# Where the softmax scale is multiplied in: from VectorE to POOL's rounding and a ScalarE copy

## The chip, the cores and the metric

The kernel runs on one core of a Trainium2 chip. TensorE (PE) multiplies matrices, VectorE (DVE), ScalarE (ACT) and GpSimd (POOL) work elementwise, and SyncE's queue (SP) issues the DMAs. The metric is the device time of one execution in microseconds (us), given as the median of several runs; one further execution was profiled.

## The reference

One layer of a streaming encoder over 1024 positions of width 1024, all in float32. A normalized, modulated input is projected once; the columns feed two groups of eight attention heads, whose outputs are joined and projected again, and a gated MLP follows. Both groups end in the same two steps, here for the first of them:

```python
s = jnp.where(mask[None, None], s, NEG_INF)
p = jax.nn.softmax(s, axis=-1).astype(v.dtype)
return jnp.einsum('bhqk,bkhd->bqhd', p, v)
```

The first group (latent attention, names with m) sees all earlier chunks of 64 positions. The second (band attention, names with c) sees a band of nine chunks and adds a bias that depends on the distance.

## The kernel before

Attention is cut into tiles of 128 query rows of one head. Eight heads by eight row blocks make 64 tiles of band attention and then 64 of latent attention, in `tiles`, half a head at a time (`Unit`). `scores` makes the probabilities of a tile, `values` multiplies those of two tiles by the values, three tiles behind. Between them `pace` and `need` draw pieces of other work from `fillers`: projections of later heads, the latent up-projections and the output projection of the band heads.

For a tile, `scores` does this, in order:

- TensorE writes the negated scores into one of two score banks (lines 822 and 829).
- VectorE takes the row minimum (840 and 844 for band tiles, which also adds the bias; 847 for latent ones).
- ScalarE takes the exponential into `P`, with the row sum in `rsum` as accumulator output (854). It appears in the profile as an activation and an accumulator read.
- VectorE takes the reciprocal `ri` of the sum (856) and multiplies it in place by `PSCALE`, 2 to the 15th (857).
- The probabilities, times `ri`, are split into two float16 halves side by side in `hl`. POOL rounds the product to the high half (`scale_pool`, line 74, called from the branch `mode == "1"`, which both mode strings choose for every piece). VectorE forms the product again and subtracts the high half, which leaves the low one (876). A latent tile of more than 512 columns is split in two pieces, so there are 64 band and 96 latent roundings.
- A DMA issued by SyncE transposes `hl` into `PT` (888), which `values` reads (916). Line 925 and 926 then join the two halves of the result.

`P` has three buffers, `hl` four and `rsum`, `ri` and `m` four each, one column wide.

The program is written in one stream. A planner orders it when the kernel is built: it plays the instructions through a model of their times and puts each engine's instructions into the order in which they come up there, by dependence and priority. Scores, the scaling and rounding, and the values each get a raised priority (`OFF_S`, `OFF_P`, `OFF_V`). On the chip every engine keeps the order that was written for it and waits where an input isn't ready.

Of the kernel before, what the change touches and what calls it, by code (L numbers as in the profile page):

```python
# [13 lines left out]
F32 = mybir.dt.float32  # L14
# [4 lines left out]
AF = mybir.ActivationFunctionType  # L19
# [3 lines left out]
MUL, ADD, SUB, MIN, MAX = ALU.mult, ALU.add, ALU.subtract, ALU.min, ALU.max  # L23

P = 128
# [21 lines left out]
PSCALE, VSCALE = 2.0 ** 15, 2.0 ** 14  # L47
# [18 lines left out]
def layer_kernel(ctx, tc, I, out):  # L66
    nc = tc.nc
    pe, act, dve, pool, sp = nc.tensor, nc.scalar, nc.vector, nc.gpsimd, nc.sync
# [4 lines left out]
    def scale_pool(o, i, s):  # L73
        pool.tensor_scalar(o, i, s, 1.0, op0=MUL, op1=MUL)  # L74
# [12 lines left out]
    cst = ctx.enter_context(tc.tile_pool(name="cst", bufs=1))  # L87
# [60 lines left out]
    def pgtile(shape, dt, name):  # L148
        return apg.tile(shape, dt, name=name, tag="pg", bufs=6)
# [642 lines left out]
    class Unit:  # L792
# [7 lines left out]
        def scores(u, i):  # L800

            qpg, kpgs = u.pages()
            bias = u.bias() if u.band else None
            lo = max(0, i - 4) if u.band else 0
            n = (i - lo + 1) * P
            nm = f"{u.nm}_{i}"
            rsum = cst.tile([P, 1], F32, name=f"rs{nm}", tag="rsum", bufs=4)
            ri = cst.tile([P, 1], F32, name=f"ri{nm}", tag="ri", bufs=4)
            with tc.high_priority(offset=OFF_S):
                s = ps.tile([P, 1024], F32, name=f"s{nm}", tag="S", bufs=2)  # L810
                n0 = max(0, min(4, i + 1) - lo) * P
                n1 = n - n0
                c0 = 512 - n0 if n1 else 0
                segs = [(c0, lo * P, n0, 0)] if n0 else []
                if n1:
                    segs.append((512, max(lo, 4) * P - 512, n1, 1))
                q = slice((i % 4) * P, (i % 4 + 1) * P)
                if u.band:
                    qh, ql = qpg
                    for x, a in enumerate((qh[u.odd], ql[u.odd])):  # L820
                        for c, ko, w, kh in segs:
                            last = pe.matmul(s[:, c:c + w], a[:, q], kpgs[kh][:, u.odd, ko:ko + w],
                                             start=(x == 0), stop=(x == 1))
                else:
                    for a in range(2):
                        for c, ko, w, kh in segs:
                            for b in range(2 - a):
                                rr = slice(0, QK if a or b else QK + NT)
                                last = pe.matmul(s[:, c:c + w], qpg[a][rr, q], kpgs[kh][rr, b, ko:ko + w],  # L829
                                                 start=(a == 0 and b == 0), stop=(a == 1))  # L830
                trail.append(last.ins)
                sv = s[:, c0:c0 + n]
                m = cst.tile([P, 1], F32, name=f"m{nm}", tag="m", bufs=4)
                if u.band:
                    if i >= 4:
                        dve.memset(sv[64:128, 0:64], BIG)
                    w = min(n, 256)
                    if n > 256:
                        m0 = cst.tile([P, 1], F32, name=f"m0{nm}", tag="m0", bufs=4)
                        dve.tensor_reduce(m0[:], sv[:, :n - 256], axis=AX.X, op=MIN)  # L840
                        init = m0[:]
                    else:
                        init = 3e38
                    anchor["dve"] = dve.tensor_tensor_reduce(sv[:, n - w:n], sv[:, n - w:n], bias[:, 256 - w:256], 1.0, init,  # L844
                                             ADD, MIN, accum_out=m[:]).ins
                else:
                    anchor["dve"] = dve.tensor_reduce(m[:], sv, axis=AX.X, op=MIN).ins  # L847
                short = n <= (640 if u.band else 512)
                pieces = [(0, n)] if short else [(0, 512), (512, n)]
                if n <= 640:  # L850
                    pr = at.tile([P, 640], F32, name=f"P{nm}", tag="P", bufs=P_BUFS)
                else:
                    pr = pgtile([P, 1024], F32, f"P{nm}")
                act.activation(pr[:, :n], sv, AF.Exp, bias=m[:], scale=-1.0, accum_out=rsum[:, 0:1])  # L854
            with tc.high_priority(offset=OFF_P):
                dve.reciprocal(ri[:], rsum[:, 0:1])
                dve.tensor_scalar(ri[:], ri[:], PSCALE, None, op0=MUL)  # L857
                for x, (p0, p1) in enumerate(pieces):
                    w = p1 - p0
                    cnt[0] += 1  # L860
                    if not u.band and cnt[0] % 4 == 0:
                        hl = apg.tile([P, 1024], F16, name=f"hl{nm}_{x}", tag="v16", bufs=3)
                    else:
                        hl = at.tile([P, 1280], F16, name=f"hl{nm}_{x}", tag="HL", bufs=HL_BUFS)
                    pp = pr[:, p0:p1]
                    mode = (MODE_C if u.band else MODE_M)[cnt[0] % 4]
                    if mode == "2":
                        scale_pool(pp, pp, ri[:])
                        act.activation(hl[:, :w], pp, AF.Copy)
                        pool.tensor_tensor(hl[:, w:2 * w], pp, hl[:, :w], op=SUB)  # L870
                    else:
                        if mode == "1":
                            scale_pool(hl[:, :w], pp, ri[:])
                        else:
                            act.activation(hl[:, :w], pp, AF.Copy, scale=ri[:])
                        dve.scalar_tensor_tensor(hl[:, w:2 * w], pp, ri[:], hl[:, :w], op0=MUL, op1=SUB)  # L876
                    nb = 10 if u.band else 8
                    if i % 2 == 0:
                        pair[0] += 1
                        if u.band or pair[0] % 2:  # L880
                            tt = at.tile([P, 20, P], F16, name=f"PT{nm}_{x}", tag="PT", bufs=2)
                        else:
                            tt = apg.tile([P, 16, P], F16, name=f"PT{nm}_{x}", tag="v16", bufs=3)
                        u.pt[i, x] = tt, {}
                    tt, where = u.pt[i - i % 2, x]
                    b0 = (i % 2) * nb
                    with tc.issue_after(anchor["om"]) if u is units[-1] and i == 7 else contextlib.nullcontext():
                        anchor["sp"] = sp.dma_start_transpose(tt[:, b0:b0 + 2 * w // P, :], hl[:, :2 * w]).ins
                    for j in range(w // P):
                        where.setdefault(lo + p0 // P + j, []).append((b0 + j, b0 + j + w // P, i % 2))  # L890
            return sum(3 * max(107, w / 2.4) for _, _, w, _ in segs)
# [789 lines left out]
```

## Time and profile before

| | us |
|---|---|
| median of 3 runs | 1311.97 |
| lowest and highest | 1311.38, 1319.53 |
| profiled execution, its own time | 1312.59 |
| span in the profile | 1310.8 |
| TensorE busy | 1189.1 (91%) |
| VectorE busy | 1075.0 (82%) |
| ScalarE busy | 625.8 (48%) |
| POOL busy | 597.9 (46%) |

In the profile a line names engine, source line, output and inputs; buffer numbers are left out, so `hlc` stands for the `hl` tiles of band attention and `hlm` for those of latent attention, `ric` and `rim` for their reciprocals. "PEld" is the loading of weights into TensorE. In a group, the count is followed by busy time and mean duration in ns, and then by the idle time of the engine just before such instructions, with what ended it. In a timeline each line gives the start and the duration in us. PEclk is the clock granted to TensorE as a share of its full speed.

### The profile page before, as it was taken

The numbers are of one execution on the slowest core, as the hardware profiler recorded it, in microseconds if no ns is written. First come the engines' busy times: TensorE is split into PE (matmuls) and PEld (weight loads), VectorE is DVE, ScalarE is ACT, GpSimd is POOL, SyncE is SP. The second block draws the span as 40 slices with busy tenths as digits, with TensorE's granted clock in tenths as the row PEclk, the third lists the DMA queues.
The fourth block names the chain that finished last, engine by engine and source line by source line (L and its number), as shares of the span: only waits on it lengthen the run. The fifth ranks groups of instructions, "written<-read, shape, count | busy, mean of one in ns | idle before, by whom it ended". The sixth has DMA issues, their size and how long they took to land. (4 is left out here: it accounts for less than half of the span.)

```text
span 1310.8 us, 18660 instructions
## 1 busy us (share of the span) xinstructions
PE 1189.1 (91%) x6168; PEld 988.0 (75%) x6168; DVE 1075.0 (82%) x1800; ACT 625.8 (48%) x1148; POOL 597.9 (46%) x639
## 2 busy tenths in 40 slices
PE   3899998889767889878989999999999999999998
PEld 3789888878545667656778888888888886888886
DVE  6979988888589778875899889888888987687667
ACT  5454654455567454543474443444453353433331
POOL 5485773587688534445515444544445441000000
PEclk9899999989889998988999999999999999999999
DMA  8416758766224777679503333343333337943451
GB/s 323 150 50 154 177 141 189 158 161 123 51 70 85 161 162 149 147 161 357 231 0 112 97 125 116 119 128 107 105 121 111 122 105 267 395 135 102 129 161 64
DMA packets 223688, 190.82 MB, mean 146 GB/s; under 512 B 148708, under 2 KB 166372, under 8 KB 223592
## 3 DMA queue, kind: packets, MB, share of 16 engines
q1 hardware_dynamic: 223592, 189.64, 51.4%
q8 instruction: 48, 0.79, 0.3%
q14 instruction: 48, 0.39, 0.1%
HBM read 117.50 MB, written 37.49 MB: 118 GB/s over the span
## 5 line engine op out<-in xcount | busy, mean ns | idle before, releaser
L78 ACT ACTIVATE dnP<-dnr 128x1024 fp32r<-128x1024 f32 x73 | 77.5, 1065 | 116.3 <-PE dnA_P L1492 46.3
L1464 DVE TENSOR_TENSOR dnP<-dnr,dnP 128x1024 fp32r<-128x1024 f32 x72 | 88.3, 1230 | 51.3 <-ACT dnP L78 51.3
L74 POOL TENSOR_SCALAR hlm<-Pm,rim 128x512 f16<-128x512 f32 (+3 forms) x96 | 67.5, 712 | 73.4 <-DVE rim L857 20.2
L85 POOL TENSOR_TENSOR wf<-wu,wf 128x512 fp32r<-128x512 f32 x22 | 39.6, 1798 | 116.6 <-ACT wf L78 116.6
L85 POOL TENSOR_TENSOR wb<-wu,wb 128x512 fp32r<-128x512 f32 x22 | 43.8, 1993 | 84.8 <-ACT wb L78 57.1
L876 DVE SCALAR_TENSOR_TENSOR hlm<-Pm,rim,hlm 128x512 f16<-128x512 f32 (+3 forms) x96 | 72.3, 769 | 12.4 <-POOL hlm L74 12.1
L829 PE MATMUL sm<-kp,qp 96*128 96x512 f32 (+7 forms) x288 | 70.0, 370 | 10.8 <-ACT Pm L854 7.7
L1326 DVE SCALAR_TENSOR_TENSOR u<-c,cvp,u 128x1023 f32<-128x1023 f32 x44 | 55.8, 1310 | 27.6 <-ACT u L1325 26.2
L854 ACT ACTIVATE Pm<-sm,mm 128x128 f32<-128x128 f32 (+3 forms) x64 | 47.3, 740 | 44.7 <-DVE mm L847 35.4
L74 POOL TENSOR_SCALAR hlc<-Pc,ric 128x640 f16<-128x640 f32 (+2 forms) x64 | 48.8, 765 | 42.8 <-DVE ric L857 14.7
L854 ACT ACTIVATE Pc<-sc,mc 128x640 f32<-128x640 f32 (+2 forms) x64 | 42.3, 662 | 51.4 <-DVE mc L844 28.6
L829 PEld LDWEIGHTS sm<-kp,qp 96*128 96x128 f32 (+1 forms) x288 | 48.0, 195 | 21.9 <-ACT Pm L854 12.3
L1325 ACT ACTIVATE u<-c,cvp 128x1024 f32<-128x1024 f32 x44 | 52.4, 1240 | 23.4 <-DVE c L1424 16.5
L916 PE MATMUL pvm<-PTm,vt 128*128 128x256 f16 (+1 forms) x320 | 42.6, 279 | 19.7 <-DMA PTm<-hlm 17.1
L876 DVE SCALAR_TENSOR_TENSOR hlc<-Pc,ric,hlc 128x640 f16<-128x640 f32 (+2 forms) x64 | 52.5, 827 | 8.5 <-POOL hlc L74 8.3
L78 ACT ACTIVATE wc<-ws 128x512 fp32r<-128x512 f32 x21 | 13.3, 634 | 92.9 <-DVE ws L1174 87.1
L1327 DVE SCALAR_TENSOR_TENSOR u<-c,cvp,u 128x1022 f32<-128x1022 f32 x44 | 55.5, 1302 | 0.0
L155 PE MATMUL ipq<-wq_s,hT 128*128 128x256 f32 x192 | 55.5, 289 | 0.0
L916 PEld LDWEIGHTS <-vt 128*128 128x128 f16 x320 | 30.1, 103 | 33.3 <-issue 20.5
L157 PE MATMUL ipq<-wq_s,hT 128*128 128x256 f32 x192 | 54.6, 284 | 0.0
L156 PE MATMUL ipq<-wq_s,hT 128*128 128x256 f32 x192 | 54.6, 284 | 0.0
L1491 PE MATMUL dnA_P<-dnP 128*128 128x512 f32 x132 | 51.3, 389 | 0.0
(436 smaller groups left out, 4376.0 us busy)
## 6 DMA issues: line engine op xcount, KB each, us to landing
wu<-w_up SPq DMA_DIRECT2D x44, 512.0 KB, 3.6
dnr<-g_d SPq DMA_DIRECT2D x73, 256.0 KB, 2.8
aw<-w_ada SPq DMA_DIRECT2D x48, 256.0 KB, 3.2
g_d<-u SPq DMA_DIRECT2D x22, 512.0 KB, 3.0
dnr<-w_down SPq DMA_DIRECT2D x44, 256.0 KB, 5.4
adaw<-w_ada_a SPq DMA_DIRECT2D x16, 512.0 KB, 6.4
x<-x SPq DMA_DIRECT2D x16, 512.0 KB, 9.1
g_d<-gs SPq DMA_DIRECT2D x22, 256.0 KB, 2.8
```

The lines of the kernel that those rows point to most:

```text
L74: pool.tensor_scalar(o, i, s, 1.0, op0=MUL, op1=MUL)
L78: act.activation(o, i, AF.Copy)
L85: (pool if eng == "p" else dve).tensor_tensor(o, i, f32(hi), op=SUB)
L155: pe.matmul(pt, sh, mh, start=(start and i == 0), stop=False)
L156: pe.matmul(pt, sh, ml, start=False, stop=False)
L829: last = pe.matmul(s[:, c:c + w], qpg[a][rr, q], kpgs[kh][rr, b, ko:ko + w], start=(a == 0 and b == 0), stop=(a == 1))
L854: act.activation(pr[:, :n], sv, AF.Exp, bias=m[:], scale=-1.0, accum_out=rsum[:, 0:1])
L876: dve.scalar_tensor_tensor(hl[:, w:2 * w], pp, ri[:], hl[:, :w], op0=MUL, op1=SUB)
L916: last = pe.matmul(dst, u.vst(j), mov, start=(x == 0), stop=(x == len(todo) - 1), skip_group_check=True)
L1326: dve.scalar_tensor_tensor(u[:, 1:], c[:, :S - 1], cvp[:, cv + 1:cv + 2], u[:, 1:], op0=MUL, op1=ADD)
L1327: dve.scalar_tensor_tensor(u[:, 2:], c[:, :S - 2], cvp[:, cv:cv + 1], u[:, 2:], op0=MUL, op1=ADD)
L1464: r = f(*a, **k)
```

## The change

The scale is no longer multiplied into `ri` by VectorE. POOL's rounding takes the unscaled reciprocal and, as its second factor, the constant `PSCALE` in place of 1.0. ScalarE copies `ri` times `PSCALE` into a new one-column tile `rp` with four buffers, and VectorE's low halves read `rp` in place of `ri`. Since the constant is a power of two, both orders of multiplying give the same numbers.

```diff
             with tc.high_priority(offset=OFF_P):
                 dve.reciprocal(ri[:], rsum[:, 0:1])
-                dve.tensor_scalar(ri[:], ri[:], PSCALE, None, op0=MUL)
+                rp = cst.tile([P, 1], F32, name=f"rp{nm}", tag="rp", bufs=4)
+                act.activation(rp[:], ri[:], AF.Copy, scale=PSCALE)
...
                         if mode == "1":
-                            scale_pool(hl[:, :w], pp, ri[:])
+                            pool.tensor_scalar(hl[:, :w], pp, ri[:], PSCALE, op0=MUL, op1=MUL)
                         else:
                             act.activation(hl[:, :w], pp, AF.Copy, scale=ri[:])
-                        dve.scalar_tensor_tensor(hl[:, w:2 * w], pp, ri[:], hl[:, :w], op0=MUL, op1=SUB)
+                        dve.scalar_tensor_tensor(hl[:, w:2 * w], pp, rp[:], hl[:, :w], op0=MUL, op1=SUB)
```

## The prediction

> **What bounds the kernel now.** I read the span and engine shares first, then busy time by stage, since an average over 1310.8 us hides that the change acts only while attention runs.
>
> ```profile
> span 1310.8 us, 18660 instructions
> ```
>
> ```profile
> core 0: us, PE busy (x) PEld busy (x) DVE busy (x) ACT busy (x) POOL busy (x), PEclk, DMA share, GB/s
> 80.00:345.00 265.00, 237.07 (x1713) 218.85 (x1712) 221.59 (x623) 138.84 (x354) 174.63 (x254) 0.96 0.65 149
> 345.00:600.00 255.00, 206.18 (x1080) 156.87 (x1079) 204.97 (x461) 139.60 (x321) 148.03 (x171) 0.92 0.62 130
> 600.00:1311.00 711.00, 693.00 (x3033) 564.68 (x3032) 584.64 (x592) 310.13 (x412) 230.49 (x158) 0.99 0.43 144
> ```
>
> The stretches are band attention, latent attention, and all that follows. From 600 us on TensorE is busy for 693 of 711 us: nothing there is won by an attention edit. Over 80 to 600 us it is busy 443 of 520 us, so 77 us of TensorE idle is the most that any shortening here could win. VectorE is next, 427 us (82%); POOL has 323 (62%), ScalarE 278 (54%). So the edit moves work from the second-busiest engine to the least busy of the four, which counts only where TensorE is waiting in the end. The waits say how often that is:
>
> ```profile
> ACT Pm L854 <- DVE mm L847: 35.4, 21, 3.9
> ...
> ACT Pc L854 <- DVE mc L844: 28.6, 20, 4.5
> ...
> PE pvm L916 <- DMA PTm<-hlm: 17.1, 11, 5.7
> ...
> DVE hlm L876 <- POOL hlm L74: 12.1, 18, 1.7
> ...
> PE pvc L916 <- DMA PTc<-hlc: 9.8, 8, 2.5
> ...
> DVE hlc L876 <- POOL hlc L74: 8.3, 8, 2.9
> ...
> PE sc L822 <- ACT Pc L854: 7.9, 7, 2.7
> PE sm L829 <- ACT Pm L854: 7.7, 9, 2.0
> ```
>
> (Columns: total us, times, longest.) TensorE waits 17.1 + 9.8 = 26.9 us for the transposes, which end the chain that the edit shortens: exponential, reciprocal, scale, POOL's rounding, VectorE's low halves, transpose. That is 35% of its 77 us. It waits 7.9 + 7.7 = 15.6 us (20%) for an exponential to release a score bank, which the edit can lengthen. I use these two shares as rates at which time won on VectorE, or lost on ScalarE, reaches the end. That is a choice: a rate is one only if the engine's time is passed on in full at those waits and not at the others.
>
> One band tile shows the chain in order of time:
>
> ```profile
> 260.30 0.19 ACT L854 ACTIVATION_READ_ACCUMULATOR Pc<-sc,mc 128x1 f32 x1
> ...
> 260.40 0.59 ACT L350 ACTIVATE raw<-ipq 128x512 f32<-128x512 f32 x1
> ...
> 261.02 0.63 ACT L352 ACTIVATE sq<-raw 128x512 f32<-128x512 f32 x1
> ...
> 261.28 0.15 DVE L856 RECIPROCAL ric<-rsc 128x1 f32<-128x1 f32 x1
> ...
> 262.73 0.14 DVE L857 TENSOR_SCALAR ric<-ric 128x1 f32<-128x1 f32 x1
> 262.79 0.74 DVE L461 SCALAR_TENSOR_TENSOR aacc<-aw,cs,aacc 128x512 f32<-128x512 f32 x1
> ...
> 263.04 1.17 POOL L74 TENSOR_SCALAR hlc<-Pc,ric 128x640 f16<-128x640 f32 x1 [3.20 <-PE q_ps L749]
> ...
> 264.57 1.01 DVE L876 SCALAR_TENSOR_TENSOR hlc<-Pc,ric,hlc 128x640 f16<-128x640 f32 x1
> ```
>
> The reciprocal is done at 261.43, but other VectorE work sits between it and its scale, so POOL starts at 263.04; POOL is done at 264.21 and VectorE takes up the low halves only at 264.57.
>
> **The change part by part.**
>
> *VectorE's scale goes.*
>
> ```profile
> L857 DVE TENSOR_SCALAR ric<-ric x64: 120/148/156, 89.6 to 328.3; 128x1 f32<-128x1 f32 x64
> L857 DVE TENSOR_SCALAR rim<-rim x64: 124/145/155, 373.0 to 585.9; 128x1 f32<-128x1 f32 x64
> ...
>   POOL hlm L74: 20.2, 12
>   POOL hlc L74: 14.7, 9
> ```
>
> There are 128 of these. By duration they hold 64 x 0.148 + 64 x 0.145 = 18.8 us. But the next instruction starts 0.06 us after the scale does (262.73, then 262.79), so the queue gets back 128 x 0.06 = 7.7 us. I take 7.7 and keep 18.8 as the bound.
>
> *POOL starts from the reciprocal.* POOL waited last for the scale 21 times, 34.9 us. In the tile above it could start some 1.3 us sooner (263.04 followed the scale's end, 262.87, by 0.17; the reciprocal's end plus 0.17 is 261.60, so up to 1.4). Yet VectorE's low halves then had 0.36 us of queue in front of them. What reaches VectorE is at most its own waits for POOL, 12.1 + 8.3 = 20.4 us in 26 of 160 roundings. I take half of it, 10.2, since in the tile shown nothing would be won and the waits were not all caused by the scale; bounds 0 and 20.4.
>
> *POOL's second multiplication.*
>
> ```profile
> L74 POOL TENSOR_SCALAR hlm<-Pm,rim 128x512 f16<-128x512 f32 (+3 forms) x96 | 67.5, 712 | 73.4 <-DVE rim L857 20.2 <-ACT Pm L854 16.1 <-DMA PTm<-hlm 15.1
> L74 POOL TENSOR_SCALAR hlc<-Pc,ric 128x640 f16<-128x640 f32 (+2 forms) x64 | 48.8, 765 | 42.8 <-DVE ric L857 14.7 <-issue 10.0 <-ACT sq L352 5.5
> ```
>
> Line 74 already multiplies twice, by the reciprocal and by 1.0; now the second factor is the constant. Same form, same operands: 0 us.
>
> *ScalarE's copy comes.* The nearest rows are a copy of 4 columns and what follows it:
>
> ```profile
> L684 ACT ACTIVATE kraw<-ssr 128x4 f32<-128x4 f32 x16 | 3.3, 205 | 0.0
> ```
>
> ```profile
> 406.32 0.21 ACT L684 ACTIVATE kraw<-ssr 128x4 f32<-128x4 f32 x1
> 406.42 0.48 ACT L689 ACTIVATE vt<-ku,vabm 128x256 f16<-128x256 f32 x1
> ```
>
> 128 x 0.205 = 26.2 us busy; the next instruction starts 0.10 us later, so 128 x 0.10 = 12.8 us of queue. I take 12.8. The exponentials already share the engine with copies, so I charge no reload of the function table.
>
> *The new waits.* The copy waits for the reciprocal with all of ScalarE's queue behind it: the next exponential, the query/key page copies and the projections' evacuations, and through them TensorE (score banks) and VectorE (minima come before exponentials, low halves after the copy). In the tile above the wait would be nothing if the planner puts the copy behind line 352 (ends 261.65, reciprocal ready 261.43), and 261.43 - 260.49 = 0.94 us if it stands directly behind the accumulator read. The planner knows the dependence and had work to put there; ScalarE also stood idle 64 us in all before exponentials, for minima. I take 0.08 us a tile, 10 us, between 0 and 128 x 0.94 = 120 us. VectorE's low halves now wait for the copy as well as for POOL; a rounding lasts 0.71 to 0.77 us on average, against 0.205 for the copy, so I charge nothing; if ScalarE is inside an exponential that cover is gone, and the cost is part of the same 10 us.
>
> Sum: gain 0.35 x (7.7 + 10.2) = 6.3 us; loss 0.20 x (12.8 + 10) = 4.6 us. That nets -1.7 us, of which the sign is not safe. To it I add the one place where the chain lies bare, the end of attention:
>
> ```profile
> 582.51 0.15 DVE L856 RECIPROCAL rim<-rsm 128x1 f32<-128x1 f32 x1
> ...
> 584.23 0.14 DVE L857 TENSOR_SCALAR rim<-rim 128x1 f32<-128x1 f32 x1
> ...
> 585.19 0.16 DVE L856 RECIPROCAL rim<-rsm 128x1 f32<-128x1 f32 x1
> ...
> 585.86 0.15 DVE L857 TENSOR_SCALAR rim<-rim 128x1 f32<-128x1 f32 x1
> ...
> 586.66 2.51 PE L916 MATMUL pvm<-PTm,vt 128*128 128x256 f16 x12 [5.73 <-DMA PTm<-hlm]
> ...
> 592.93 3.36 PE L916 MATMUL pvm<-PTm,vt 128*128 128x256 f16 x16 [3.76 <-DMA PTm<-hlm]
> ```
>
> TensorE stands 5.73 + 3.76 us there. The two last tiles' scales follow their reciprocals by 1.72 and 0.67 us; what ends the stage is the last one, so 0.7 us. Total -2.4 us. The profiled run took 1312.59 us, 1.8 us more than its span and 0.6 above the median of the three runs (1311.97): 1312.6 - 2.4 = 1310.2 for a run like the profiled one, 1309.6 against the median. I forecast 1310. The other times below are counted from the median, 1312.
>
> [...] Two neighbouring roundings:
>
> ```profile
> 304.12 0.80 POOL L74 TENSOR_SCALAR hlc<-Pc,ric 128x640 f16<-128x640 f32 x1 [0.17 <-DVE ric L857]
> ```
>
> ```profile
> 304.96 0.88 DVE L876 SCALAR_TENSOR_TENSOR hlc<-Pc,ric,hlc 128x640 f16<-128x640 f32 x1
> 305.10 1.41 POOL L74 TENSOR_SCALAR hlc<-Pc,ric 128x640 f16<-128x640 f32 x1 [0.18 <-issue]
> ```
>
> The one beside a low-halves instruction took 0.61 us longer. [...] An earlier rounding meets other VectorE work than now; this is the third rival.
>
> **The rivals.**
>
> *ScalarE blocked (slower), 0.24.* The reciprocal sits behind VectorE work that the planner thought shorter, and the copy stands at ScalarE's head. Priced at the full 0.94 us of the tile shown: 120 us of standing, of which 20% reaches TensorE, 24 us; with 2.6 for the copies themselves and 6.3 + 0.7 gained, 1312 + 19.6 = 1331.6. It passes 1% from about 0.68 us a tile. For it: ScalarE feeds everybody here. Against: 46% of ScalarE's time in these stretches is idle.
>
> *VectorE and the chain were the bound (faster), 0.21.* All 18.8 and 20.4 us come back at 35%, 13.7 us, and 0.7 at the end of attention, with ScalarE's additions hidden in its idle time: 1312 - 14.4 = 1297.6. For it: 82% and 64 us of exponentials late for minima, which an emptier VectorE would bring sooner.
>
> *Collisions on the shared port, 0.09.* If half of the 160 roundings grew by 0.61 us, 49 us of POOL at the rate of 35%, 17 us, less the 2.4 gained: 1326.6. Against: nothing in the edit makes collisions likelier than now; each early rounding may also leave one.
>
> *Nothing reaches the end, 0.12.* TensorE's queue is full and the planner refills the gap: 1312.
>
> **Numbers.** The forecast (1310) has 0.34. Its own range is 1300 to 1320: at the low end VectorE's two gains stand at their bounds and nothing waits for the reciprocal (1312 - 13.7 - 0.7 + 2.6), at the high end only the 7.7 us of queue come back, the copies cost 26.2 and the wait is 0.25 us a tile, 32 us (1312 - 2.7 - 0.7 + 0.2 x 58). A measurement of this kernel tells about 1%, 13 us, from no change. Faster by over 1% means below 1298.9: the faster rival, 0.21, whose price lies just beyond, so 0.20 with the little that the forecast's tail adds and the rival's near side takes off. Slower means above 1325.1: nearly all of the blocked rival, 0.21, and half of the port rival, 0.04: 0.25. Within: 0.55. The range 1295 to 1331 takes in the faster rival's price and the blocked one from 0.68 almost up to 0.94 us a tile.
>
> **What would show it.** Line 857 gone and 128 one-column copies on ScalarE, about 0.2 us each; POOL's waits for VectorE (34.9 us) falling by half or more; VectorE busy some 19 us less up to 600 us. Right: the stage after attention starts 1 to 5 us sooner. Blocked rival: ScalarE idle ahead of the new copies, released by the reciprocal, and longer TensorE waits for exponentials. Port rival: the mean of line 74's roundings above 0.71 and 0.77 us. I am wrong altogether if the planner's order past 600 us changes and TensorE's 693 of 711 us there moves.

## The result: 0.6% slower

The changed kernel took 1321.87 us in the median (1316.97 to 1324.44, 16 runs); the kernel before, run beside it, 1315.05 us (1308.59 to 1321.92, 16 runs). The ratio is 1.0059, with a 95% interval of [1.0042, 1.0075]: some 8 us slower, where 2.4 us faster was forecast. The time lies inside the range of 1295 to 1331 us, but the interval of the ratio lies wholly above 1: the kernel did become slower, where it was to become faster. (The kernel before was at 1311.97 in the three runs that the prediction knew.)

In the groups of the changed kernel (busy time and mean ns of one; then the engine's idle time just before, and what ended it) the edit is all there:

```profile
L874 POOL TENSOR_SCALAR hlm<-Pm,rim 128x512 f16<-128x512 f32 (+3 forms) x96 | 72.3, 762 | 70.2 <-DVE rim L856 38.2 <-DMA PTm<-hlm 26.6 <-issue 4.1
...
L874 POOL TENSOR_SCALAR hlc<-Pc,ric 128x640 f16<-128x640 f32 (+2 forms) x64 | 48.2, 756 | 48.9 <-DVE ric L856 36.1 <-issue 6.0 <-DMA aw<-w_ada 4.8
...
L854 ACT ACTIVATE Pc<-sc,mc 128x640 f32<-128x640 f32 (+2 forms) x64 | 42.1, 659 | 48.0 <-DVE mc L844 34.2 <-POOL hlc L874 3.1 <-POOL wq_s L85 2.8
...
L858 ACT ACTIVATE rpc<-ric 128x1 f32<-128x1 f32 x64 | 12.7, 199 | 23.2 <-DVE ric L856 22.1 <-DVE vsc L330 0.3
...
L858 ACT ACTIVATE rpm<-rim 128x1 f32<-128x1 f32 x64 | 11.8, 197 | 16.2 <-DVE rim L856 15.6
```

VectorE's line 857 is gone, ScalarE has 128 copies of 0.2 us, and POOL's roundings (now line 874) wait for the reciprocal itself. But those waits are 38.2 + 36.1 = 74.3 us, where 34.9 stood before and at most half of that was expected. The idle time ahead of all roundings hardly moved: 70.2 + 48.9 = 119.1 us against 73.4 + 42.8 = 116.2. In this kernel POOL stands as long as it did, and more of it is put down to VectorE.

The busy time by stage, in the stretches used before:

```profile
span 1318.5 us, 18630 instructions
```

```profile
80.00:345.00 265.00, 232.36 (x1700) 215.87 (x1698) 216.69 (x547) 144.63 (x412) 173.96 (x253) 0.96 0.65 147
345.00:600.00 255.00, 202.80 (x1070) 156.40 (x1071) 202.13 (x406) 146.47 (x384) 152.97 (x171) 0.91 0.57 121
600.00:1318.00 718.00, 698.59 (x3060) 569.98 (x3057) 600.95 (x595) 312.66 (x418) 232.48 (x160) 0.99 0.44 147
```

(Columns after the stretch's length: busy PE, PEld, VectorE, ScalarE, POOL, each with its count; clock, DMA share, GB/s.) Up to 600 us VectorE is busy 216.69 + 202.13 = 418.8 us, 7.7 less than 426.6. TensorE, too, did less by the same moments: 1700 matmuls instead of 1713 in band attention, 232.36 us of work instead of 237.07. Over the whole span it worked 1185.7 us instead of 1189.1, so the loss is idle time, 1318.5 - 1185.7 = 132.8 us against 121.7.

Where it arose is seen in two landmarks of TensorE, the first matmul of latent attention's query projection (`qu`) and the last of its scores (`sm`); the two times in each row are the first and the last start. Before:

```profile
L155 PE MATMUL qu<-wq,latT x32: 391/400/774, 341.8 to 417.9; 128*128 128x512 f32 x32
```

```profile
L829 PE MATMUL sm<-kp,qp x288: 218/390/776, 367.5 to 579.7; 104*128 104x512 f32 x38, 96*128 96x512 f32 x37, 96*128 96x128 f32 x19, 104*128 104x128 f32 x16
```

After:

```profile
L155 PE MATMUL qu<-wq,latT x32: 393/397/774, 349.8 to 427.7; 128*128 128x512 f32 x32
```

```profile
L829 PE MATMUL sm<-kp,qp x288: 218/392/628, 375.3 to 584.6; 96*128 96x512 f32 x39, 104*128 104x512 f32 x39, 104*128 104x128 f32 x16, 104*128 104x384 f32 x16
```

Latent attention starts 8.0 us late (349.8 against 341.8), as much as the whole span lost (7.7 us). That points at band attention, but doesn't show it yet: the lag is 4.9 us at the last scores (584.6 against 579.7) and 10.6 us where the output projection begins (606.91 against 596.3). Each landmark comes from one profiled execution, and executions of one kernel differ by up to 13 us (1308.59 to 1321.92 before), so a difference of a few us between two landmarks is a hint only.

One more thing changed that the diff doesn't show. The planner, given other instructions, wrote another order for every engine. Compared by the longest order that the two programs have in common, TensorE has 683 of its 6128 instructions in another place, VectorE 347 of 1600, ScalarE 119 of 965, POOL 89 of 636 and SyncE 88 of 682 (counted in the programs, not in the trace). Of TensorE's 683, 339 are among the 1995 instructions up to the end of band attention. A late spot in band attention shows the difference:

```profile
211.75 0.47 DVE L424 SCALAR_TENSOR_TENSOR v<-ipv,vabc,v 128x256 f16<-128x256 f32 x1
...
212.15 0.87 DVE L877 SCALAR_TENSOR_TENSOR hlc<-Pc,rpc,hlc 128x640 f16<-128x640 f32 x1
...
213.12 0.15 DVE L856 RECIPROCAL ric<-rsc 128x1 f32<-128x1 f32 x1
213.14 0.46 DVE L424 SCALAR_TENSOR_TENSOR v<-ipv,vabc,v 128x256 f16<-128x256 f32 x1
213.36 0.80 POOL L874 TENSOR_SCALAR hlc<-Pc,ric 128x640 f16<-128x640 f32 x1 [2.07 <-DVE ric L856]
...
213.91 0.79 DVE L461 SCALAR_TENSOR_TENSOR aacc<-aw,cs,aacc 128x512 f32<-128x512 f32 x1 [0.31 <-DMA aw<-w_ada]
...
214.75 1.05 PE L474 MATMUL p_ada<-ones,aacc 128*128 128x1 f32 x8 [2.42 <-DVE aacc L461]
```

POOL begins 0.09 us after its reciprocal ends, as the edit means it to. TensorE stands 2.42 us, for an accumulation (`aacc`, filler work) that VectorE's queue took up behind two evacuations (line 424), low halves and the reciprocal, and then 0.31 us late for its weight. In the trace of before the weight load of such a product waits once for line 461, 0.17 us (at 208.84), and its matmul not at all; here the weight load waits 2.56 us in the same moment as the matmul its 2.42.

### The profile page after: what moved, and what is told of

Same layout as the page of the kernel before. It is cut to its first block, busy times and chain, and to the rows that moved or that the text cites. A ratio compares the mean times of both kernels' runs of the same rounds, so it can differ in the third digit from the quotient of the medians.

```text
span 1318.5 us, 18630 instructions
## 1 busy us (share of the span) xinstructions
PE 1185.7 (90%) x6168; PEld 988.7 (75%) x6168; DVE 1083.9 (82%) x1672; ACT 640.7 (49%) x1276; POOL 603.7 (46%) x639
## 4 chain that ended last, share of the span: by engine, by line
PE 49%; DVE 3%; issue 1%; DMA 1%; ACT 1%; POOL 1%; SPq 0%; POOLq 0%; ACTq 0%
PE p L1158 10%; PE p L1157 10%; PE p L1156 10%; PE dnA_P L1491 2%; PE dnA_P L1492 2%; PE dnA_P L1493 2%; PE dnB_P L1491 2%; PE dnB_P L1492 2%; PE dnB_P L1493 2%; PE op L155 1%; PE op L156 1%; PE dnA L1491 1%; PE dnA L1492 1%; PE dnA L1493 1%; PE dnB L1492 1%
## 5 line engine op out<-in xcount | busy, mean ns | idle before, releaser
L1465 DVE TENSOR_TENSOR dnP<-dnr,dnP 128x1024 fp32r<-128x1024 f32 x72 | 88.5, 1231 | 51.1 <-ACT dnP L78 51.1
L874 POOL TENSOR_SCALAR hlm<-Pm,rim 128x512 f16<-128x512 f32 (+3 forms) x96 | 72.3, 762 | 70.2 <-DVE rim L856 38.2
L85 POOL TENSOR_TENSOR wf<-wu,wf 128x512 fp32r<-128x512 f32 x22 | 38.8, 1765 | 116.3 <-ACT wf L78 110.4
L1327 DVE SCALAR_TENSOR_TENSOR u<-c,cvp,u 128x1023 f32<-128x1023 f32 x44 | 62.7, 1464 | 27.6 <-ACT u L1326 27.6
L877 DVE SCALAR_TENSOR_TENSOR hlm<-Pm,rpm,hlm 128x512 f16<-128x512 f32 (+3 forms) x96 | 69.9, 749 | 11.9 <-POOL hlm L874 11.5
L874 POOL TENSOR_SCALAR hlc<-Pc,ric 128x640 f16<-128x640 f32 (+2 forms) x64 | 48.2, 756 | 48.9 <-DVE ric L856 36.1
L1328 DVE SCALAR_TENSOR_TENSOR u<-c,cvp,u 128x1022 f32<-128x1022 f32 x44 | 68.9, 1604 | 0.0
L877 DVE SCALAR_TENSOR_TENSOR hlc<-Pc,rpc,hlc 128x640 f16<-128x640 f32 (+2 forms) x64 | 52.2, 824 | 7.6 <-POOL hlc L874 7.4
L847 DVE TENSOR_REDUCE mm<-sm 128x1 f32<-128x128 f32 (+3 forms) x64 | 47.1, 745 | 11.3 <-PE sm L829 11.0
```

The source lines that it names most:

```text
L85: (pool if eng == "p" else dve).tensor_tensor(o, i, f32(hi), op=SUB)
L874: pool.tensor_scalar(hl[:, :w], pp, ri[:], PSCALE, op0=MUL, op1=MUL)
L877: dve.scalar_tensor_tensor(hl[:, w:2 * w], pp, rp[:], hl[:, :w], op0=MUL, op1=SUB)
L1465: r = f(*a, **k)
```

## The experiments

Two theories could explain the loss. **The edit**: the copies hold ScalarE up, or a wait took the place of the one removed. **The order**: the edit itself is worth what the prediction summed, and the planner's new order costs more. To tell them apart, the order was fixed. A chain of edges that carry no semaphores, only sequence, holds each engine's instructions to a given list; the instructions that the edit adds are left out of it and go where they come up.

```diff
         layer_kernel(ctx, tc, I, out)
+        pin_order(tc)
```

```python
# pin_order, for each engine's list: i follows prev
tc.add_manual_dep(i, prev.name, mybir.DependencyInfo(
    mybir.DependencyClass.NoSync, mybir.DependencyReason.DATA), reason="pin")
```

### The edit and the order, each alone

First the changed kernel in the order of before, then the code of before in the order of the changed kernel.

> The change as it is, but every engine keeps the order of the kernel before; only the 128 ScalarE copies are put in where they come up. If the loss of 0.59% lies in the instructions themselves (the copy's wait, its 26 us on ScalarE), this is slower than before by about as much, 1.004 to 1.008. If it lies in the order that the planner laid for the changed kernel, this is at 0.997 to 1.002, with the gain of the sum (2 us) if that was right.

> The kernel before, scale on VectorE and all, but every engine keeps the order of the changed kernel; only the 128 scales are put in where they come up. If the order is what costs, 1.004 to 1.008. If the instructions are what costs, 0.998 to 1.002.

The edit in the old order: **0.9975 [0.9955, 0.9995]**, 1310.4 us beside 1313.31. The old code in the new order: **1.0161 [1.0128, 1.0194]**, 1334.13 us. So the order is the loss, 0.84% with the edit in it (1.0059 / 0.9975 = 1.0084) and 1.6% without, which is twice what was expected. The edit gains in both: 0.25% in the old order, 1.0% in the new (1.0059 / 1.0161 = 0.990). The figure for the new order also holds what it costs that the 128 scales were put into an order laid without them.

With the order held, the tile of the prediction can be met again. The edit in the old order:

```profile
260.15 0.59 ACT L350 ACTIVATE raw<-ipq 128x512 f32<-128x512 f32 x1
...
260.78 0.15 DVE L856 RECIPROCAL ric<-rsc 128x1 f32<-128x1 f32 x1
260.96 0.20 ACT L858 ACTIVATE rpc<-ric 128x1 f32<-128x1 f32 x1 [0.22 <-DVE ric L856]
261.03 0.80 POOL L874 TENSOR_SCALAR hlc<-Pc,ric 128x640 f16<-128x640 f32 x1 [2.92 <-DVE ric L856]
261.07 0.61 ACT L352 ACTIVATE sq<-raw 128x512 f32<-128x512 f32 x1
261.52 0.84 DVE L461 SCALAR_TENSOR_TENSOR aacc<-aw,cs,aacc 128x512 f32<-128x512 f32 x1 [0.59 <-DMA aw<-w_ada]
...
264.54 0.88 DVE L877 SCALAR_TENSOR_TENSOR hlc<-Pc,rpc,hlc 128x640 f16<-128x640 f32 x1
```

POOL starts 0.25 us after the reciprocal starts (261.03 - 260.78); before it was 1.76 (263.04 - 261.28). Yet VectorE takes up the low halves at 264.54, before at 264.57: the 1.5 us that POOL won end in VectorE's queue. And in VectorE's queue the freed place ends in a wait of 0.59 us for a weight from the DMA. The copy went in front of line 352 and held ScalarE up for 0.22 us.

In the groups of this run POOL's roundings start earlier, as the prediction hoped, but VectorE's low halves gain next to nothing from it, and the copies wait longer than it took:

```profile
L877 DVE SCALAR_TENSOR_TENSOR hlm<-Pm,rpm,hlm 128x512 f16<-128x512 f32 (+3 forms) x96 | 69.2, 739 | 13.1 <-POOL hlm L874 9.2 <-ACT rpm L858 3.4
...
L877 DVE SCALAR_TENSOR_TENSOR hlc<-Pc,rpc,hlc 128x640 f16<-128x640 f32 (+2 forms) x64 | 50.8, 799 | 6.9 <-POOL hlc L874 6.7
...
L874 POOL TENSOR_SCALAR hlm<-Pm,rim 128x512 f16<-128x512 f32 (+3 forms) x96 | 70.9, 746 | 63.8 <-DVE rim L856 31.9 <-DMA PTm<-hlm 26.7 <-DVE hlm L877 3.0
...
L874 POOL TENSOR_SCALAR hlc<-Pc,ric 128x640 f16<-128x640 f32 (+2 forms) x64 | 50.4, 790 | 28.2 <-DVE ric L856 21.7 <-issue 2.1 <-PE pvc L917 1.7
...
L858 ACT ACTIVATE rpc<-ric 128x1 f32<-128x1 f32 x64 | 12.4, 198 | 19.3 <-DVE ric L856 16.6 <-DVE vsc L327 1.2 <-DVE vsc L332 0.6
...
L858 ACT ACTIVATE rpm<-rim 128x1 f32<-128x1 f32 x64 | 12.1, 197 | 10.3 <-DVE rim L856 9.7
```

POOL's idle time ahead of all roundings is 63.8 + 28.2 = 92.0 us, 24.2 less than the 116.2 of before, so the earlier start shows there; in the changed kernel, with the new order, it was 119.1. The low halves wait 9.2 + 6.7 = 15.9 us for POOL, 4.5 less than the 20.4 of before, but the latent ones now wait 3.4 us for the copy. All of VectorE's idle time ahead of low halves is 13.1 + 6.9 = 20.0 us, and was 20.9 (12.4 and 8.5 in the groups of before). The copies stand 16.6 + 9.7 = 26.3 us for their reciprocal. In the tile above ScalarE's queue stood with them: line 352 reads what line 350 had finished at 260.74, and it starts at 261.07, behind the copy that waited for the reciprocal.

The waits by which the gain was to reach TensorE did not shrink with the time. Before, TensorE waited 26.9 us for the transposes. With the order held, where the kernel is faster (total us, times, longest):

```profile
PE pvm L917 <- DMA PTm<-hlm: 23.1, 13, 6.2
...
PE pvc L917 <- DMA PTc<-hlc: 7.0, 7, 2.5
```

And in the changed kernel, which is slower:

```profile
PE pvm L917 <- DMA PTm<-hlm: 11.1, 9, 2.1
...
PE pvc L917 <- DMA PTc<-hlc: 7.2, 11, 1.1
```

That is 30.1 and 18.3 us. By which waits the 0.25% is gained stays open.

### Each half of the edit

The POOL half: POOL multiplies by the reciprocal and the constant, and VectorE still makes the scaled reciprocal, in a tile of its own.

```diff
-                dve.tensor_scalar(ri[:], ri[:], PSCALE, None, op0=MUL)
+                rp = cst.tile([P, 1], F32, name=f"rp{nm}", tag="rp", bufs=4)
+                dve.tensor_scalar(rp[:], ri[:], PSCALE, None, op0=MUL)
...
-                            scale_pool(hl[:, :w], pp, ri[:])
+                            pool.tensor_scalar(hl[:, :w], pp, ri[:], PSCALE, op0=MUL, op1=MUL)
...
-                        dve.scalar_tensor_tensor(hl[:, w:2 * w], pp, ri[:], hl[:, :w], op0=MUL, op1=SUB)
+                        dve.scalar_tensor_tensor(hl[:, w:2 * w], pp, rp[:], hl[:, :w], op0=MUL, op1=SUB)
```

The copy half: ScalarE makes it, and POOL and VectorE both read it.

```diff
-                dve.tensor_scalar(ri[:], ri[:], PSCALE, None, op0=MUL)
+                rp = cst.tile([P, 1], F32, name=f"rp{nm}", tag="rp", bufs=4)
+                act.activation(rp[:], ri[:], AF.Copy, scale=PSCALE)
...
-                            scale_pool(hl[:, :w], pp, ri[:])
+                            scale_pool(hl[:, :w], pp, rp[:])
...
-                        dve.scalar_tensor_tensor(hl[:, w:2 * w], pp, ri[:], hl[:, :w], op0=MUL, op1=SUB)
+                        dve.scalar_tensor_tensor(hl[:, w:2 * w], pp, rp[:], hl[:, :w], op0=MUL, op1=SUB)
```

Both in the order of before:

> Only the first half of the change, in the order of the kernel before: POOL starts from the reciprocal and multiplies by the constant, and VectorE still makes the scaled copy, into a tile of its own. If the earlier start is worth something (10 us on VectorE at a rate of 35%, as in the sum), 0.996 to 0.999; if POOL's later work and VectorE's queue hide it, 0.999 to 1.001. POOL's waits for VectorE ahead of the roundings should fall from 35 us to under 20 if the scale was what it waited for, and stay where the reciprocal was.

> Only the second half, in the order of the kernel before: ScalarE makes the scaled copy, and both POOL and VectorE read it; POOL multiplies by 1.0 as before. If ScalarE's copy is late (behind an exponential, or waiting for the reciprocal with the queue behind it), this is the dearest of the four, 1.004 to 1.010, since POOL now waits for it too; if it is not, 0.998 to 1.002.

And both as the planner orders them:

> Only POOL's half of the change (scaled copy still on VectorE), planned freely. No ScalarE copy, so nothing of its wait; but the planner's order moves as much as for the whole change. If the order is what decides, this lies off the 1.003 that the same code had in the old order, by 0.5% or more, either way. If it is within 0.3% of it, the planner's orders are about equal and the order of the changed kernel was an unlucky one.

> ScalarE's copy of the whole row sum's reciprocal with POOL's old multiplication by it, planned freely. In the order of before this half took 1.0052. If a freely planned order costs what it cost the whole change (0.84%): about 1.0136. If it gives what it gave the POOL half (from 1.003 to 0.9975): about 0.9997. The distance between the two readings is what the planner's order scatters for edits of this size.

| | order of before | planned freely |
|---|---|---|
| POOL half | 1.003 [1.0007, 1.0053] | 0.9975 [0.9958, 0.9993] |
| copy half | 1.0052 [1.0028, 1.0075] | 1.0086 [1.0058, 1.0113] |
| whole edit | 0.9975 [0.9955, 0.9995] | 1.0059 [1.0042, 1.0075] |

In the order of before neither half gains, and the whole does. ScalarE's copy alone lengthens the way to POOL, which then waits 55.7 + 32.3 = 88.0 us for the copies. The POOL half is slower than both of its expected ranges. POOL's waits for VectorE, which were to fall under 20 us if it was the scale that POOL waited for, are 38.8 + 26.2 = 65.0 us, now for the reciprocal. POOL's idle time ahead of all roundings does fall, to 66.7 + 32.4 = 99.1 us; why the kernel is slower all the same wasn't found. Free planning takes 0.55% off the POOL half and adds 0.84% to the whole edit; for the copy half it adds 0.34% by the middles, but the intervals overlap. The order is thus not a cost of this edit that could be priced by its instructions; it goes either way, by about as much as any part of the edit is worth. The last expectation had named 1.0136 and 0.9997 as its two ends; 1.0086 lies between them.

### What the copy's wait is worth

In the order of before, the copy takes a column that is ready from the start, so it waits for no reciprocal:

```diff
-                act.activation(rp[:], ri[:], AF.Copy, scale=PSCALE)
+                act.activation(rp[:], ones[:, 0:1], AF.Copy, scale=PSCALE)
```

> The change in the old order, but ScalarE's copy reads a column of ones in place of the reciprocal, so it waits for nothing; the low halves are then of a product with the constant instead of the row's reciprocal. What it gains on the change in the old order (0.9975) is the price of the copy's wait. By the sum (10 us of waiting at a rate of 20%) 2 us, so 0.995 to 0.998; if the waits are hidden, 0.997 to 0.999; if the blocked-queue rival was right, under 0.99.

The low halves are then formed with the constant alone; this kernel leaves the reciprocal out of them. It took 0.9956 [0.9942, 0.997], against 0.9975 [0.9955, 0.9995] for the whole edit in the old order: about 2.5 us less by the two middles, with intervals that overlap.

But ScalarE did not stop standing, as the groups of this run show:

```profile
L858 ACT ACTIVATE rpm<-ones 128x1 f32<-128x1 f32 x64 | 12.6, 200 | 33.8 <-DVE hlm L877 29.8 <-DVE hlc L877 3.1 <-DVE rim L856 0.6
...
L858 ACT ACTIVATE rpc<-ones 128x1 f32<-128x1 f32 x64 | 12.0, 197 | 26.6 <-DVE hlc L877 26.2
```

With an input that is always ready, the copies run ahead (ScalarE has 68 instructions in the first 80 us, 63 in the edit in the old order) and then stand for one of the four buffers of `rp`, until VectorE's low halves have read it: 33.8 + 26.6 = 60.4 us of idle time ahead of copies, where the edit with its wait had 19.3 + 10.3 = 29.6. So the experiment doesn't price the wait for the reciprocal, which it was made for. It shows something else: twice the standing of ScalarE, at other places in its queue, and a kernel that is no slower.

### The end of attention

In the changed kernel, ScalarE stood 10.17 us for a weight of the output projection, with TensorE's first matmul of that projection behind it:

```profile
604.35 0.63 ACT L78 ACTIVATE wo<-wor 128x512 fp32r<-128x512 f32 x1 [10.17 <-DMA wor<-w_out]
...
606.91 0.79 PE L155 MATMUL op<-wo,oh 128*128 128x512 f32 x1 [3.90 <-ACT oh L78]
```

So this load was planned earlier:

```diff
-    wo = [load_wo(0, n, "a", "v" if n else "p") for n in range(2)]
+    with tc.high_priority(offset=100):
+        wo = [load_wo(0, n, "a", "v" if n else "p") for n in range(2)]
```

> The changed kernel, planned anew with one thing more: the loads of the last output-projection weights (line 704) have a raised priority, so that SyncE's queue holds them ahead of the last transposes. In the changed kernel they left at 599.6 us, ScalarE stood 10.2 us in front of their rounding, and the next stage began 4.2 us after the last value product (0.3 us in the kernel before). If that wait is on the path, 4 to 6 us less than the changed kernel: 1.000 to 1.003 against before. If something else ends that stage, 1.005 to 1.007 as the changed kernel.

1.005 [1.0037, 1.0064]: no gain that can be told from 1.0059. The wait only changed its name. In that run:

```profile
595.56 0.63 ACT L78 ACTIVATE wo<-wor 128x512 fp32r<-128x512 f32 x1 [2.21 <-DMA wor<-w_out]
...
607.85 0.63 ACT L78 ACTIVATE oh<-ol 128x512 fp32r<-128x512 f32 x1 [9.82 <-DMA ol<-oT_d]
```

The weight is there at 595.56, and ScalarE then stands 9.82 us for the attention result, which comes no sooner (the first such load is issued at 603.0 us, in the changed kernel at 600.6).

### Which part of the new order costs

Four kernels hold only the order of band attention; everything after it is planned freely, from whatever state that leaves. The edit is whole in each.

> The changed kernel, its band attention in the order of the kernel before, everything later planned freely (which gives a third order there). If the order of the band stage costs the 4 to 8 us that the landmarks show (last projection product 7.7 us late, first latent product 8.0), the last band scores and the first latent products come 2 to 4 us earlier than in the kernel before, and the total is 0.998 to 1.003, by what the third order makes of the rest. If the loss came from the instructions after all, the band stage ends as late as in the changed kernel.

> The changed kernel, in which TensorE alone keeps the issue order of the kernel before in the stage of band attention (to about 345 us); the other engines and the later stages are planned freely. Theory A, the loss lies in the order of TensorE's matmuls in this stage: ratio 0.996 to 0.999 as with all engines' order kept (0.9975). Theory B, the loss lies in the order of VectorE, ScalarE or POOL: ratio near the changed kernel's, 1.004 to 1.008, last band-stage row product some 8 us late. Theory C, every new order lands where chance puts it, and the one planned after 345 us counts as much: anything from 0.995 to 1.012, with no link to the landmark at 345 us.

> The changed kernel, in which all engines but TensorE keep the issue order of the kernel before in the stage of band attention; TensorE and the later stages are planned freely. Theory A (TensorE's order is what costs): ratio 1.004 to 1.008. Theory B (the other engines' order costs): 0.996 to 0.999. Theory C (chance): anything from 0.995 to 1.012.

> The changed kernel, in which VectorE alone keeps the issue order of the kernel before in the stage of band attention. VectorE serves the late accumulations for which TensorE idled longest in the changed kernel (2.42 us in front of one product). If VectorE's order is what costs: ratio 0.996 to 0.999. If it is TensorE's: 1.004 to 1.008. If chance: anything from 0.995 to 1.012.

| kept in the order of before, in band attention | ratio | first `qu`, us |
|---|---|---|
| nothing (the changed kernel) | 1.0059 [1.0042, 1.0075] | 349.8 |
| TensorE alone | 1.0084 [1.0056, 1.0113] | 353.8 |
| VectorE alone | 1.0038 [1.0019, 1.0058] | 345.2 |
| all engines | 0.9975 [0.996, 0.999] | 340.0 |
| all but TensorE | 0.9927 [0.9902, 0.9952] | 338.7 |

(The kernel before has 341.8 there.) Holding the order of band attention alone makes good the whole loss, and holding TensorE's alone makes good nothing of it: a new order of VectorE, ScalarE, POOL and SyncE is enough to cost what was lost. The best row is not one with a new order on TensorE, though. With the other four held, the planner left only 35 of TensorE's 1995 instructions of this stage out of their old places (339 in the changed kernel, counted in the programs). So up to the end of band attention the last two rows are almost the same program, and whether a new order of TensorE would cost anything by itself wasn't tested. That row, at 0.9927, is also better than any reading had it. VectorE's order alone brings back 4.6 of the 8.0 us at the landmark, in one profiled execution, while its ratio, just below what was expected if VectorE's order didn't matter, can't be told from the changed kernel's; how the rest falls on the other three wasn't tried.

The groups agree. With TensorE alone in the old order:

```profile
L874 POOL TENSOR_SCALAR hlc<-Pc,ric 128x640 f16<-128x640 f32 (+2 forms) x64 | 50.0, 784 | 54.2 <-DVE ric L856 42.8 <-issue 4.9 <-PE ipv L157 2.7
...
L854 ACT ACTIVATE Pc<-sc,mc 128x640 f32<-128x640 f32 (+2 forms) x64 | 42.0, 658 | 44.3 <-DVE mc L844 38.0 <-DVE vsc L323 2.1 <-DVE modT L478 1.6
```

With all but TensorE:

```profile
L854 ACT ACTIVATE Pc<-sc,mc 128x640 f32<-128x640 f32 (+2 forms) x64 | 42.2, 660 | 42.3 <-DVE mc L844 21.9 <-DVE hlc L877 7.5 <-POOL hlc L874 2.7
...
L874 POOL TENSOR_SCALAR hlc<-Pc,ric 128x640 f16<-128x640 f32 (+2 forms) x64 | 49.7, 780 | 30.8 <-DVE ric L856 21.5 <-DMA aw<-w_ada 3.4 <-issue 2.8
```

In the changed kernel and with TensorE alone held, the band tiles' exponentials wait 34 to 38 us for VectorE's minima and POOL 36 to 43 us for its reciprocals; with the other engines held, 22 us each. VectorE comes later to the chain of the tiles. The waits and the time don't always go together, so this reading is not shown: with VectorE alone held the minima are waited for 23.2 us, the reciprocals still 38.7, and the stage is 3.4 us late. The freely planned POOL half has 35.6 and 51.1 us of these waits and starts latent attention 9.6 us late, as this reading would have it, but it makes that up in latent attention (last `sm` at 579.6) and ends at 0.9975. Why the planner puts VectorE's work so, and which single displacement is to blame, stays open.

The best version is 0.7% faster than the kernel before: 1303.21 us in the median, 1301.14 to 1308.54 in 9 runs. Its two landmarks are:

```profile
L155 PE MATMUL qu<-wq,latT x32: 392/397/774, 338.7 to 416.7; 128*128 128x512 f32 x32
```

```profile
L829 PE MATMUL sm<-kp,qp x288: 220/393/796, 362.9 to 569.0; 96*128 96x512 f32 x38, 104*128 104x512 f32 x38, 104*128 104x128 f32 x16, 96*128 96x128 f32 x16
```

Of its lead in the profile only 3.1 us are there when latent attention begins (338.7 against 341.8); 10.7 are there at its end (569.0 against 579.7). That stage was planned freely, so nearly 8 us come from an order that nobody chose, as the changed kernel's loss did. The row with all engines held has almost the same order in band attention and starts latent attention within 1.3 us of it (340.0), but its last scores start at 577.6. What parts the two, 0.9927 and 0.9975, thus arose mostly after band attention, where both were planned freely.

## Why the prediction was wrong

**The step that failed** is one that the sum didn't have. All terms were set against the order of before, as if the planner would put its instructions where they stood. Of the order it said only "I am wrong altogether if the planner's order past 600 us changes"; in a rival, "the planner refills the gap" was a reason for no change. The order changed from band attention on, and cost 1.0084, some 11 us, more than four times the sum. A term for the order should have stood there with bounds on both sides, though nothing in the trace of before gives its size.

**The sum.** -2.4 us was forecast; the edit in the old order gave 0.9975 [0.9955, 0.9995], of 1313.31 us -3.3 [-5.9, -0.7]. Sign and size were right for the edit alone, but its terms and rates were not borne out, so the agreement of the totals is in part luck. The rate of 35% rested on TensorE's waits for the transposes, and these did not fall when the kernel gained (30.1 us against 26.9).

- VectorE's scale gone: up to 600 us VectorE was to be busy some 19 us less. It is 7.7 less in the changed kernel and 14.7 with the order held (217.43 + 194.47 = 411.9 us); other work had moved into these stretches. The 7.7 us of its queue as such wasn't measured.
- POOL's earlier start, 10.2 us at a rate of 35%: the tile shown says nothing is won there, and it stayed so (264.54 against 264.57). By itself, with VectorE's scale kept, the earlier start gave 1.003 in the order of before; the two gains can't be had one at a time, so the split of 7.7 and 10.2 isn't confirmed. In the order of before VectorE's waits for POOL fell by 4.5 us and all its idle time ahead of low halves by 0.9, where 10.2 was taken. That POOL had waited for the scale in the tile shown, as the prediction read it, is borne out, although the profile puts that wait down to TensorE (`q_ps`).
- POOL's second multiplication at nothing: the mean of the latent roundings rose from 712 to 762 ns, that of the band ones fell from 765 to 756. In the freely planned POOL half they are 708 and 750, so the constant as such costs nothing. In the order of before the whole edit has 746 and 790; why they are longer there (34 x 96 + 25 x 64 ns = 4.9 us of POOL) wasn't tried.
- The copies: 0.2 us each, no reload of the function table (5 loads of 1283 ns in the changed kernel, 5 before), and the next instruction 0.10 us after the start, as here in the edit in the old order:

```profile
407.73 0.19 ACT L858 ACTIVATE rpm<-rim 128x1 f32<-128x1 f32 x1
407.83 0.47 ACT L854 ACTIVATE Pm<-sm,mm 128x256 f32<-128x256 f32 x1
```

- The copy's wait: 10 us of standing at a rate of 20%, 2 us, was taken. It stood 26.3 us for the reciprocals (37.7 in the changed kernel), 2.6 times as long. What that cost isn't known. The rate isn't borne out either: 60.4 us of standing instead of 29.6 should by it have cost 0.20 x 30.8 = 6.2 us, and that kernel was no slower.
- The end of attention, -0.7 us: not seen by itself.

**The rivals.** ScalarE blocked: one of its signs is there, 37.7 us of idle time ahead of the copies, 42 times, released by the reciprocal. The other is not: TensorE's waits for exponentials to release a score bank are 6.6 + 9.3 = 15.9 us, 15.6 before. Nor is the price: with 29.6 us of standing the edit gains in the order of before, and with 60.4 the kernel is no slower. VectorE and the chain as the bound: in the order of before no, the edit gives 0.25%, not 1.1%. (In the new order it gave 1.0%, but that figure also holds the placing of the 128 scales.) Collisions: this rival needed 49 us more in the roundings; the sums of line 874 are 72.3 + 48.2 = 120.5 us against 116.3 before. What lengthens such a rounding, a port or something else, no run shows. That some are longer, the timelines show for the 30 band roundings of 128x640 that stand there singly: before, the 16 that overlap VectorE's TENSOR_TENSOR and SCALAR_TENSOR_TENSOR instructions by over 0.3 us last 1.02 us on average and the other 14 0.81; in the changed kernel these are 17 with 1.03 us and 13 with 0.80, so hardly more collide. Nothing reaches the end: no, 0.9975 lies below 1, narrowly.

**The signs named.** Line 857 and the copies: right. POOL's waits for VectorE halved: wrong, 53.6 us in the old order and 74.3 in the new; the name of the last releaser had said less than it seemed, since the reciprocal was late too. The stage after attention 1 to 5 us sooner: true of the edit alone in the old order (591.9 against 596.3), 10.6 us later in the changed kernel (606.91). From there to the end of the span it took 711.6 us, before 714.5; that this stretch would move was to be the test of being "wrong altogether", and it was the wrong one.

## What to carry to other kernels

Where a planner orders the instructions, a small edit is two changes: its own, and a new order for everything around it. Hold the order fixed to measure the edit alone, and give the order a term of its own in the forecast, with both signs; here it spread over more than 1%, several times what the edit was worth. Time that an engine stands for the operation that was removed isn't time won: look at what that engine's next wait, and its reader's queue, would be.

## What the runs showed that was not expected

ScalarE, with half its time free, stood 29.6 us ahead of its copies in one kernel and 60.4 in another with the same order on the other engines, and the second was no slower (0.9975 and 0.9956, intervals overlapping). And the order of the busiest engine was not the one to hold: with TensorE's old order alone the kernel stands at 1.0084, no better than the changed kernel; with that of the four less busy engines alone it stands at 0.9927, and TensorE's old order came back with it, but for 35 of 1995 instructions.
